# Causal attention in a hybrid decoder kernel: where the transposed queries, the keys and the values are split into two parts

## The chip, the core and the metric

The kernel runs on one core of a Trainium2 chip. A core has TensorE (matrix products and transposes, results in PSUM), VectorE, ScalarE and GpSimd (element-wise work), and SyncE, which issues DMAs here. The metric is the device time of one execution in microseconds. Before the change three runs took 1360.54 us in the median, 1357.71 to 1362.46.

## The reference

Two layers, 1024 tokens, model width 1024. In each layer one input projection feeds a convolution branch, an attention branch and a gated mixing branch; their outputs are gated, normalised, joined and projected. The change touches the attention alone:

```
def _causal_attention(q, k, v):          # 8 heads, q and k 96 wide, v 64 wide
    for each block of 128 queries:
        s = einsum(q_block, k) * Dq ** -0.5
        s = where(k_pos <= q_pos, s, -inf)
        p = softmax(s)
        out = einsum(p, v)
```

All arithmetic is float32. The kernel gets that from a TensorE format of less precision by writing an operand as hi + lo, hi being the rounded value and lo the rest (x - hi), and summing two or three products.

## The kernel before

The layers run one after the other. In a layer come the input projection with the convolution and mixing branches, the latent projections, keys and values per token (`ksb`, `vsb`), queries per token (`qsb`), attention head by head, and the output projection.

Attention of head h needs the queries and keys with their 96 channels on partitions. `qk_part` does it in four parts (keys or queries, first or second 512 tokens): four transposes on TensorE into a PSUM bank `qkt`, then the split into `qT` and `kT`. Before the change a part goes through three engines: ScalarE copies the bank to an SBUF tile `qkraw` (two buffers; L1022 for queries, L1024 with a gain for keys), VectorE casts `qkraw` to hi (L1025), GpSimd subtracts hi from `qkraw` for lo (L1026). `v_split` splits the 64 value columns of a head for all 1024 tokens into `vh`: VectorE casts hi (L1005), GpSimd subtracts (L1007).

Then `score` forms the scores `s` of a block of 128 queries in one of two double banks, VectorE takes the row maximum (L1050), ScalarE the exponential into `p` (L1056). `ptrans` transposes `p` into a bank `pt`, which ScalarE and VectorE split into `pT` (L169, L170): `pT_400` is head 4, first half of its queries, first 128 keys. `pv` sums the products with `vh` in a bank `o`; `os` (L1100, L1101) and `ot` bring the sum back to tokens. GpSimd also multiplies the gate `zsm` by one over the softmax's sum (L1076). The banks `qkt`, `pt`, `o` and `ot` come from one pool of four.

The order of the program is made by a planner in `attention`: it keeps a clock of TensorE and estimates (`est`) when ScalarE and VectorE are through, and takes up what it believes is ready. `t_ready` is when it believes a part of `qT` or `kT` to be usable. Work of the next head is placed between the scores of this one. The framework's scheduler may still move instructions of an engine past each other. On the chip every engine works off its own list in order.

Of the kernel before, what the change touches and what calls it, by code (L numbers as in the profile page):

```python
# [19 lines left out]
P = 128  # L20
# [21 lines left out]
# Columns of the input projection: where each part starts.  # L42
# [3 lines left out]
# Units of the input projection, in the order of their use.  # L46
# [15 lines left out]
# Pieces of the weight stream of a layer: (name, k chunks, columns).  # L62
# [11 lines left out]
# Columns of the per-partition parameters.  # L74
# [3 lines left out]
# Parameters that are rows, the same for all partitions.  # L78
# [3 lines left out]
# Columns of the constants.  # L82
# [4 lines left out]
class Flow:  # L87
    """Order of the program: work that waits for other engines is put off by as much
    tensor engine time as those take, so that engines, which run in order, find it ready."""
# [37 lines left out]
def hybrid_trunk(ctx, tc, x, w, pc, pr, sgw, pww, cst, out):  # L127
# [39 lines left out]
    def split(hi, lo, src):  # L167
        """hi + lo = src, for a source in PSUM."""
        nc.scalar.copy(hi, src)  # L169
        nc.vector.tensor_tensor(out=lo, in0=src, in1=hi.bitcast(F32), op=ALU.subtract)  # L170
# [63 lines left out]
    def late_splits():  # L234
        """Steps that split the pending pieces bit by bit."""
# [17 lines left out]
    class Unit:  # L253
        """A unit's weights: get(k) gives (hi, lo); in the last group, pieces are given back."""
# [38 lines left out]
    def s0_norm(l, i, xt, ng, pool, parts=1, dst=None):  # L293
        """RMSNorm of one tile of tokens, in place if there is no dst."""
# [13 lines left out]
    def to_chan(src, dst, t0, name, halves=1):  # L308
        """Transposes one tile of tokens, splits it into dst[:, part, k, t0:t0 + 128]."""
        chan_of([src[:, k * P:(k + 1) * P] for k in range(KC)], dst, t0, name, halves)  # L310
# [35 lines left out]
    # Products of zeros that bring the tensor engine to its full clock.  # L346
# [15 lines left out]
    # ================================================================ layers  # L362
    for l in range(L):
# [11 lines left out]
        def tok(o, un, i, n, final):  # L375
            """One tile of tokens times n columns of a unit."""
# [21 lines left out]
        def chan(un, c0, half, final, name):  # L398
            """128 channels of a unit times 512 tokens."""
# [145 lines left out]
        def silu2(o, dst, shape):  # L545
            """dst = 2 * silu(o)"""
# [5 lines left out]
        def branch_out(y, i0, c0):  # L552
            """Two tiles of a gated branch (twice its value): RMSNorm with gain, to DRAM."""
# [138 lines left out]
        # rotary tables with gains  # L692
# [12 lines left out]
        def key_prep():  # L705
            """Rotated key, sums of its squares."""
# [150 lines left out]
        def early_load(i):  # L857
            sd = t1p.tile([P, 512], F32, tag="qkraw", bufs=2, name="yse")
            side_load(i, sd[:, 0:CW], sd[:, CW:])
            early_src[i] = [sd]  # L860
# [7 lines left out]
        def open_t():  # L868
# [6 lines left out]
                  bank, bank2, mm, mm3, tr, split, ident_b, mask_b,  # L875
# [43 lines left out]
        def x_load(c, i):  # L919
            if c == 1 and not last:  # L920
                # The next layer's input: its first half is written, the second comes in place.
# [56 lines left out]
def attention(nc, flow, t1p, open_t, late_splits, extra, bank, bank2, mm, mm3, tr, split, ident_b, mask_b,  # L978
              ksb, qsb, vsb, zsm, kgain, early, l):
    """Causal softmax attention; the order of the tensor engine's work follows estimates of  # L980
    when the other engines are through with what it needs. Work of before (extra) fills the
    tensor engine while the first scores are on their way."""
# [19 lines left out]
    def v_split(h):  # L1002
        vh = vhs[h] = pool["t"].tile([P, NT, 2, DV], F32R, tag="vh", bufs=2, name=f"vh{l}_{h}")
        hc = vsb[:, :, h * DV:(h + 1) * DV]
        nc.vector.tensor_copy(vh[:, :, 0, :], hc)  # L1005
        est("dve", 0.35, flow.t)
        nc.gpsimd.tensor_tensor(out=vh[:, :, 1, :], in0=hc, in1=vh[:, :, 0, :].bitcast(F32),  # L1007
                                op=ALU.subtract)

    def qk_part(h, which, half):  # L1010
# [9 lines left out]
        raw = t1p.tile([P, 512], F32, tag="qkraw", bufs=2, name="qkraw")[:DQK, :]  # L1020
        if which == "q":
            nc.scalar.copy(raw, o[:DQK, :])  # L1022
        else:
            nc.scalar.activation(raw, o[:DQK, :], AF.Identity, scale=kgain)  # L1024
        nc.vector.tensor_copy(hi, raw)  # L1025
        nc.gpsimd.tensor_tensor(out=lo, in0=raw, in1=hi.bitcast(F32), op=ALU.subtract)  # L1026
        f = est("act", 0.55, flow.t)
        b1_free.remove(min(b1_free))
        b1_free.append(f)
        t_ready[h, which, half] = est("dve", 0.35, f) + (1.5 if h else 5.0)  # L1030
# [84 lines left out]
    # Sequence of scores and of the transposes that they need.  # L1115
# [21 lines left out]
    def s_when():  # L1137
# [3 lines left out]
        if kind != "s":  # L1141
            if "t" not in pool and h > 0:
                return None
            # The values of two heads before are read until its last product.
# [166 lines left out]
```

## Time and profile before

| | |
|---|---|
| three runs: median, lowest, highest | 1360.54, 1357.71, 1362.46 us |
| profiled execution: first to last instruction | 1356.9 us |
| what the runs have around that span | 0.8 us (lowest) to 5.6 us (highest), 3.6 us in the median |
| TensorE busy | 1281.4 us, 94% |
| VectorE, ScalarE, GpSimd busy | 855.7, 527.8, 536.8 us |
| attention of layer 0, of layer 1 | about 400 to 586 us, 1066 to 1258 us |

The profiled execution left no other time of its own than its span. Busy time is what an engine spent in instructions. PEclk is the granted clock of TensorE: 1.00 is 2.4 GHz and 0.50 is 1.2 GHz, the only two levels seen.

### The profile page before, as it was taken

Reading aid. Unit: us, or ns where it says so; the run is one execution under the profiler, and the core shown is the slowest. Engines: PE = TensorE matmul, PEld = TensorE weight load, DVE = VectorE, ACT = ScalarE, POOL = GpSimd, SP = SyncE. Lnnn points to the kernel's source line nnn. Section 1 sums busy time; section 2 is a strip of 40 time slices with the busy share of each in tenths; the row PEclk is TensorE's granted clock in tenths of the full one; section 3 lists DMA queues with packets and bytes.
Section 4 is the critical chain, followed back from the end, with each engine's and each line's share of the span. In section 5 each row is a group of like instructions: output and inputs, shape, how many; then the busy total and the mean of one; then the engine's idle time right before and its main releaser. Section 6 shows DMA issues by size and latency. Waiting matters only on the chain.

```text
span 1356.9 us, 19370 instructions
## 1 busy us (share of the span) xinstructions
PE 1281.4 (94%) x7566; PEld 1118.8 (82%) x7566; DVE 855.7 (63%) x1337; ACT 527.8 (39%) x1067; POOL 536.8 (40%) x468
## 2 busy tenths in 40 slices
PE   8999989999998989999999996999999898898998
PEld 7889879888987767778898996998889777777787
DVE  7499963124778877753555999621277877777431
ACT  6311333224346765630341211533243466566300
POOL 4724623543695333110055263344357833322100
PEclk9999989999998988999999997999999888889999
DMA  7121201211110000144432112111111100000332
GB/s 283 40 63 32 82 24 59 61 49 52 32 47 17 1 1 1 32 147 126 141 111 62 32 54 76 48 47 50 48 48 49 32 1 1 1 1 24 116 101 101
DMA packets 33820, 77.88 MB, mean 57 GB/s; under 512 B 3776, under 2 KB 12352, under 8 KB 33728
## 3 DMA queue, kind: packets, MB, share of 16 engines
q1 hardware_dynamic: 33728, 76.64, 17.9%
q8 instruction: 59, 0.97, 0.3%
q14 instruction: 33, 0.27, 0.1%
HBM read 64.05 MB, written 12.58 MB: 56 GB/s over the span
## 4 chain that ended last, share of the span: by engine, by line
PE 67%; DVE 24%; issue 4%; POOL 3%; ACT 2%; DMA 0%; SPq 0%; DVEq 0%; POOLq 0%
PE po L154 13%; DVE acc L517 13%; PE cq L154 10%; PE s L154 8%; PE o L154 6%; PE pt L165 4%; PE ckv L154 3%; PE pzk L154 3%; PE qps L154 3%; PE ZM L154 3%; PE V L154 2%; PE kps L154 2%; PE vps L154 2%; PE glu L154 2%; PE a L154 2%
## 5 line engine op out<-in xcount | busy, mean ns | idle before, releaser
L213 POOL TENSOR_TENSOR w<-raw,w 128x1024 fp32r<-128x1024 f32 (+1 forms) x49 | 137.3, 2809 | 149.6 <-ACT w L210 96.1
L154 PE MATMUL po<-w,yT 128*128 128x512 f32 x768 | 184.2, 398 | 0.0
L517 DVE SCALAR_TENSOR_TENSOR acc<-yp,dpc,acc 128x1024 f32<-128x1024 f32 x120 | 183.1, 1553 | 1.4
L154 PEld LDWEIGHTS po<-w,yT 128*128 128x128 f32 x768 | 142.9, 188 | 33.4
L154 PE MATMUL s<-kT,qT 96*128 96x384 f32 (+5 forms) x576 | 153.4, 394 | 5.4 <-ACT p L1056 5.4
L154 PE MATMUL o<-pT,vh 128*128 128x512 f32 (+3 forms) x384 | 127.8, 409 | 29.1 <-DVE pT L170 28.4
L154 PE MATMUL cq<-hT,w 128*128 128x512 f32 x576 | 132.0, 390 | 0.0
L154 PEld LDWEIGHTS cq<-hT,w 128*128 128x128 f32 x576 | 107.8, 188 | 22.2
L154 PEld LDWEIGHTS s<-kT,qT 96*128 96x128 f32 x576 | 104.1, 210 | 14.6 <-ACT p L1056 7.2
L170 DVE TENSOR_TENSOR pT<-pt,pT 128x512 fp32r<-128x512 f32 x192 | 101.1, 548 | 17.8 <-ACT pT L169 17.3
L169 ACT CAST pT<-pt 128x512 fp32r<-128x512 f32 x192 | 89.3, 478 | 58.2 <-PE pt L165 41.2
L1056 ACT ACTIVATE p<-s,rs 128x128 f32<-128x128 f32 (+7 forms) x128 | 94.9, 741 | 43.3 <-DVE rs L1050 38.6
L1050 DVE TENSOR_REDUCE rs<-s 128x1 f32<-128x128 f32 (+7 forms) x128 | 95.8, 749 | 24.8 <-PE s L154 23.2
L165 PE MATMUL pt<-cst_sb,p 128*128 128x128 f32 x576 | 99.2, 287 | 4.4 <-DVE pT L170 2.3
L154 PE MATMUL qps<-w,cqT 128*128 128x384 f32 x576 | 102.3, 337 | 0.0
L154 PEld LDWEIGHTS o<-pT,vh 128*128 128x128 f32 x384 | 69.7, 207 | 38.0 <-DVE pT L170 30.9
L154 PEld LDWEIGHTS qps<-w,cqT 128*128 128x128 f32 x576 | 100.2, 188 | 0.6
L1026 POOL TENSOR_TENSOR kT<-qkraw,kT 96x512 fp32r<-96x512 f32 x32 | 41.5, 1298 | 122.0 <-DVE kT L1025 122.0
L165 PEld LDWEIGHTS pt<-cst_sb,p 128*128 128x128 f32 x576 | 69.0, 148 | 13.1 <-ACT qkraw L1024 5.0
L174 DVE SCALAR_TENSOR_TENSOR cqT<-cq,pcs,cqT 128x512 fp32r<-128x512 f32 x24 | 18.0, 749 | 94.0 <-ACT cqT L173 94.0
L210 ACT CAST w<-raw 128x1024 fp32r<-128x1024 f32 (+1 forms) x47 | 49.6, 1057 | 49.9 <-PE a L154 14.9
L154 PE MATMUL ZM<-w,hT 128*128 128x256 f32 x384 | 53.1, 300 | 8.3 <-DVE zc L549 8.3
(306 smaller groups left out, 2374.5 us busy)
## 6 DMA issues: line engine op xcount, KB each, us to landing
raw<-in_w_dram SPq DMA_DIRECT2D x64, 512.0 KB, 3.5
raw<-in_w_dram SPq DMA_DIRECT2D x12, 576.0 KB, 3.7
xt<-in_x_dram SPq DMA_DIRECT2D x8, 512.0 KB, 8.2
xr<-xmid SPq DMA_DIRECT2D x16, 256.0 KB, 2.8
out_dram<-xr SPq DMA_DIRECT2D x16, 256.0 KB, 2.0
yn<-yside SPq DMA_DIRECT2D x24, 128.0 KB, 2.9
yside<-ug SPq DMA_DIRECT2D x8, 256.0 KB, 2.2
yside<-yc SPq DMA_DIRECT2D x8, 256.0 KB, 2.1
```

The lines of the kernel that those rows point to most:

```text
L154: nc.tensor.matmul(o, lhsT=lhsT, rhs=rhs, start=start, stop=stop)
L165: nc.tensor.transpose(out=o, in_=in_, identity=ident[:k, :k])
L169: nc.scalar.copy(hi, src)
L170: nc.vector.tensor_tensor(out=lo, in0=src, in1=hi.bitcast(F32), op=ALU.subtract)
L174: nc.vector.scalar_tensor_tensor(out=lo, in0=src, scalar=gain, in1=hi.bitcast(F32), op0=ALU.mult, op1=ALU.subtract)
L210: nc.scalar.copy(wt[:, 0, :sz], raw[:, :sz])
L213: (eng or nc.gpsimd).tensor_tensor(out=wt[:, 1, :sz], in0=raw[:, :sz], in1=wt[:, 0, :sz].bitcast(F32), op=ALU.subtract)
L517: nc.vector.scalar_tensor_tensor(out=acc, in0=yp[:, j:j + S], scalar=wc, in1=acc, op0=ALU.mult, op1=ALU.add)
L1026: nc.gpsimd.tensor_tensor(out=lo, in0=raw, in1=hi.bitcast(F32), op=ALU.subtract)
L1050: nc.vector.tensor_reduce(out=sm[:, 1, t:t + 1], in_=src if nb > 1 else o[:, :wd], axis=AX.XY if nb > 1 else AX.X, op=ALU.max, negate=True)
L1056: nc.scalar.activation(pr_[:, :n].rearrange("p (b n) -> p b n", b=nb), src, AF.Exp, bias=sm[:, 1, t:t + 1], accum_out=sm[:, 0, t:t + 1])
```

## The change

A query part is now split like `pT`: ScalarE copies the PSUM bank to hi, VectorE subtracts hi from the same bank for lo. A key part is split by the helper that the latents use, which applies the gain in both steps. `qkraw` is gone (its name tag on a later load becomes `yse`). For the values, ScalarE casts hi and VectorE subtracts; GpSimd has no part in the splits. The planner's estimates follow: the bank is taken to be free after VectorE, and `t_ready` has no margin of 1.5 (5.0 for head 0) any more.

```
     def v_split(h):
...
-        nc.vector.tensor_copy(vh[:, :, 0, :], hc)
-        est("dve", 0.35, flow.t)
-        nc.gpsimd.tensor_tensor(out=vh[:, :, 1, :], in0=hc, in1=vh[:, :, 0, :].bitcast(F32),
+        nc.scalar.copy(vh[:, :, 0, :], hc)
+        nc.vector.tensor_tensor(out=vh[:, :, 1, :], in0=hc, in1=vh[:, :, 0, :].bitcast(F32),
                                 op=ALU.subtract)
+        est("dve", 0.6, est("act", 0.55, flow.t))
...
     def qk_part(h, which, half):
...
-        raw = t1p.tile([P, 512], F32, tag="qkraw", bufs=2, name="qkraw")[:DQK, :]
         if which == "q":
-            nc.scalar.copy(raw, o[:DQK, :])
+            split(hi, lo, o[:DQK, :])
         else:
-            nc.scalar.activation(raw, o[:DQK, :], AF.Identity, scale=kgain)
-        nc.vector.tensor_copy(hi, raw)
-        nc.gpsimd.tensor_tensor(out=lo, in0=raw, in1=hi.bitcast(F32), op=ALU.subtract)
-        f = est("act", 0.55, flow.t)
+            split_gain(hi, lo, o[:DQK, :], kgain)
+        f = est("dve", 0.65, est("act", 0.55, flow.t))
         b1_free.remove(min(b1_free))
         b1_free.append(f)
-        t_ready[h, which, half] = est("dve", 0.35, f) + (1.5 if h else 5.0)
+        t_ready[h, which, half] = f
```

The helpers stood there before, and line 170 and line 174 are their VectorE steps:

```
    def split(hi, lo, src):
        nc.scalar.copy(hi, src)
        nc.vector.tensor_tensor(out=lo, in0=src, in1=hi.bitcast(F32), op=ALU.subtract)

    def split_gain(hi, lo, src, gain):
        nc.scalar.activation(hi, src, AF.Identity, scale=gain)
        nc.vector.scalar_tensor_tensor(out=lo, in0=src, scalar=gain, in1=hi.bitcast(F32),
                                       op0=ALU.mult, op1=ALU.subtract)
```

Behind the change the line numbers from 1022 on are three lower. Three places of the new order matter below. VectorE where head 4 passes to head 5, before the change:

```order
L1025 CAST kT_5_4598<-qkraw 96x512
L1050 TENSOR_REDUCE rs_5_0_4849<-s_5_0_4844 128x1
L1074 RECIPROCAL rs_4_7_4733<-rs_4_7_4733 128x4
L1005 CAST vh_5_4806<-vsb_2872 128x8x64
L1025 CAST qT_5_4597<-qkraw 96x512
L1050 TENSOR_REDUCE rs_5_0_4849<-s_5_1_4866 128x1
L170 TENSOR_TENSOR pT_400_4775<-pt_400_4768,pT_400_4775 128x512
```

The same place of VectorE with the change:

```order
L174 SCALAR_TENSOR_TENSOR kT_5_4558<-qkt_5k_4693,dpc_353,kT_5_4558 96x512
L1047 TENSOR_REDUCE rs_5_0_4799<-s_5_0_4794 128x1
L1071 RECIPROCAL rs_4_7_4689<-rs_4_7_4689 128x4
L170 TENSOR_TENSOR qT_5_4557<-qkt_5q_4711,qT_5_4557 96x512
L1047 TENSOR_REDUCE rs_5_0_4799<-s_5_1_4816 128x1
L170 TENSOR_TENSOR pT_400_4727<-pt_400_4720,pT_400_4727 128x512
L1098 TENSOR_TENSOR os<-o_31_4622,os 64x512
L1006 TENSOR_TENSOR vh_5_4758<-vsb_2872,vh_5_4758 128x8x64
```

The two casts of keys and queries have become subtractions from PSUM, and the work on the values has moved behind `pT_400`. TensorE at this place, from behind the last product of head 3 on, before the change:

```order
L165 MATMUL pt_401_4785<-cst_sb,p_4_1_4614 128x128
L165 MATMUL pt_401_4785<-cst_sb,p_4_2_4654 128x128
L165 MATMUL pt_401_4785<-cst_sb,p_4_3_4674 128x128
L154 MATMUL s_5_1_4866<-kT_5_4598,qT_5_4597 128x256 x3
L154 LDWEIGHTS ident_b
L154 MATMUL s_5_1_4866<-mask_b,ident_b 128x128
L165 MATMUL pt_402_4820<-cst_sb,p_4_2_4654 128x128
L165 MATMUL pt_402_4820<-cst_sb,p_4_3_4674 128x128
L154 MATMUL s_5_2_4906<-kT_5_4598,qT_5_4597 128x384 x3
L154 LDWEIGHTS ident_b
L154 MATMUL s_5_2_4906<-mask_b,ident_b 128x128
L154 MATMUL o_40_4828<-pT_400_4775,vh_4_4549 128x512 x2
```

The same place of TensorE with the change:

```order
L154 MATMUL s_5_1_4816<-kT_5_4558,qT_5_4557 128x256 x3
L154 LDWEIGHTS ident_b
L154 MATMUL s_5_1_4816<-mask_b,ident_b 128x128
L165 MATMUL pt_401_4751<-cst_sb,p_4_1_4572 128x128
L165 MATMUL pt_401_4751<-cst_sb,p_4_2_4604 128x128
L165 MATMUL pt_401_4751<-cst_sb,p_4_3_4619 128x128
L165 MATMUL pt_402_4774<-cst_sb,p_4_2_4604 128x128
L165 MATMUL pt_402_4774<-cst_sb,p_4_3_4619 128x128
L154 MATMUL o_40_4780<-pT_400_4727,vh_4_4509 128x512 x2
L154 MATMUL s_5_2_4848<-kT_5_4558,qT_5_4557 128x384 x3
```

The score `s_5_2`, which stood ahead of the first product of head 4 (`o_40`), stands behind it now. The third place is VectorE at the start of layer 0's attention, before the change:

```order
L1005 CAST vh_0_3668<-vsb_2872 128x8x64
L1025 CAST qT_1_3671<-qkraw 96x512
L1025 CAST kT_1_3672<-qkraw 96x512
L1005 CAST vh_1_3784<-vsb_2872 128x8x64
L170 TENSOR_TENSOR pT_000_3763<-pt_000_3756,pT_000_3763 128x512
```

The same place with the change:

```order
L1006 TENSOR_TENSOR vh_0_3660<-vsb_2872,vh_0_3660 128x8x64
L170 TENSOR_TENSOR qT_1_3663<-qkt_1q_3665,qT_1_3663 96x512
L174 SCALAR_TENSOR_TENSOR kT_1_3664<-qkt_1k_3688,dpc_353,kT_1_3664 96x512
L174 SCALAR_TENSOR_TENSOR kT_1_3664<-qkt_1k_3715,dpc_353,kT_1_3664 96x512
L170 TENSOR_TENSOR qT_1_3663<-qkt_1q_3733,qT_1_3663 96x512
L1006 TENSOR_TENSOR vh_1_3768<-vsb_2872,vh_1_3768 128x8x64
L1047 TENSOR_REDUCE rs_0_7_3711<-s_0_5_3740 128x1
L170 TENSOR_TENSOR pT_000_3758<-pt_000_3751,pT_000_3758 128x512
```

Six subtractions and a row maximum stand ahead of the first `pT` there, where four casts stood.

## Rows read from the trace of the kernel before

**Rows 1.** The page's first and fourth part: busy engines, chain that ended last.

```profile
PE 1281.4 (94%) x7566; PEld 1118.8 (82%) x7566; DVE 855.7 (63%) x1337; ACT 527.8 (39%) x1067; POOL 536.8 (40%) x468
...
PE 67%; DVE 24%; issue 4%; POOL 3%; ACT 2%; DMA 0%; SPq 0%; DVEq 0%; POOLq 0%
```

**Rows 2.** Windows between the first products of successive heads, engines' busy time, granted clock.

```profile
core 0: us, PE busy (x) PEld busy (x) DVE busy (x) ACT busy (x) POOL busy (x), PEclk, DMA share, GB/s
437.20:459.65 22.45, 20.05 (x136) 16.63 (x136) 18.63 (x35) 17.00 (x42) 9.64 (x10) 1.00 0.00 1
459.65:480.77 21.12, 18.72 (x128) 15.54 (x128) 17.97 (x32) 15.11 (x34) 7.70 (x8) 1.00 0.00 1
480.77:505.03 24.26, 21.85 (x128) 17.89 (x128) 17.97 (x32) 15.12 (x34) 7.69 (x8) 0.86 0.00 1
...
1154.62:1177.30 22.68, 20.27 (x128) 16.42 (x128) 17.96 (x32) 15.12 (x34) 7.70 (x8) 0.92 0.00 1
```

**Rows 3.** TensorE's waits, layer 0 then 1: total us, times, longest.

```profile
PE o L154 <- DVE pT L170: 13.0, 7, 2.4
...
PE ot L165 <- DVE os L1101: 1.4, 1, 1.4
...
PE o L154 <- DVE pT L170: 15.4, 9, 2.4
```

**Rows 4.** Timeline, head 4 to 5: start, us, engine, work, idle before it.

```profile
500.01 0.42 DVE L1025 CAST kT<-qkraw 96x512 fp32r<-96x512 f32 x1 [0.53 <-ACT qkraw L1024]
...
500.56 0.29 DVE L1050 TENSOR_REDUCE rs<-s 128x1 f32<-128x128 f32 x1
500.65 0.57 ACT L1022 COPY qkraw<-qkt_5q 96x512 f32<-96x512 f32 x1
...
501.06 1.01 DVE L1005 CAST vh<-vsb 128x512 fp32r<-128x512 f32 x1
...
501.75 0.79 POOL L1076 TENSOR_TENSOR zsm<-zsm,rs 128x256 f32<-128x256 f32 x1
501.78 0.77 PE L154 MATMUL s<-kT,qT 96*128 96x384 f32 x3
502.00 2.05 DVE L1025 CAST qT<-qkraw 96x512 fp32r<-96x512 f32 x1
...
502.51 1.26 POOL L1007 TENSOR_TENSOR vh<-vsb,vh 128x512 fp32r<-128x512 f32 x1
...
503.97 0.41 DVE L1050 TENSOR_REDUCE rs<-s 128x1 f32<-128x256 f32 x1
...
504.30 0.67 DVE L170 TENSOR_TENSOR pT<-pt,pT 128x512 fp32r<-128x512 f32 x1
...
505.03 0.91 PE L154 MATMUL o<-pT,vh 128*128 128x512 f32 x3 [2.41 <-DVE pT L170]
```

**Rows 5.** Line 1025, casts of queries: shortest, median and longest in ns.

```profile
L1025 DVE CAST qT<-qkraw x32: 411/423/2053, 380.2 to 1223.0; 96x512 fp32r<-96x512 f32 x32
```

**Rows 6.** Groups by line and form, whole span: busy us, mean ns, idle before.

```profile
L170 DVE TENSOR_TENSOR pT<-pt,pT 128x512 fp32r<-128x512 f32 x96 | 65.2, 685 | 17.2 <-ACT pT L169 16.7
L174 DVE SCALAR_TENSOR_TENSOR cqT<-cq,pcs,cqT 128x512 fp32r<-128x512 f32 x24 | 18.0, 749 | 94.0 <-ACT cqT L173 94.0
...
L768 DVE TENSOR_TENSOR ksb<-ksb,kst 128x512 f32<-128x512 f32 x16 | 11.0, 686 | 3.8 <-POOL kst L178 3.8
...
L447 ACT CAST vn<-vg 128x512 fp32r<-128x512 f32 x8 | 5.0, 621 | 28.3 <-POOL vg L443 24.1 <-DVE rstd L425 4.2
```

**Rows 7.** Timeline, start of layer 0's attention.

```profile
410.90 0.42 DVE L1005 CAST vh<-vsb 128x512 fp32r<-128x512 f32 x1
...
414.43 1.14 DVE L170 TENSOR_TENSOR pT<-pt,pT 128x512 fp32r<-128x512 f32 x2
415.16 0.69 PE L165 MATMUL pt<-cst_sb,p 128*128 128x128 f32 x2 [2.29 <-DVE pT L170]
```

**Rows 8.** Window behind layer 0's wait for `os`, columns as in Rows 2.

```profile
580.00:600.00 20.00, 18.00 (x95) 14.56 (x94) 13.47 (x24) 8.49 (x20) 4.09 (x7) 1.00 0.51 157
```

More of the change, by code (lines that the diff above doesn't have):

```diff
@@ L857, in early_load @@
         def early_load(i):
-            sd = t1p.tile([P, 512], F32, tag="qkraw", bufs=2, name="yse")
+            sd = t1p.tile([P, 512], F32, tag="yse", bufs=2, name="yse")
             side_load(i, sd[:, 0:CW], sd[:, CW:])
@@ L874, in hybrid_trunk @@
         attention(nc, flow, t1p, open_t, late_splits, [lambda i=i: query(1, i) for i in range(2, NT)],
-                  bank, bank2, mm, mm3, tr, split, ident_b, mask_b,
+                  bank, bank2, mm, mm3, tr, split, split_gain, ident_b, mask_b,
                   ksb, qsb, vsb, zsm, dpc[:DQK, 66:67], (early_load, early_norm), l)
@@ L975, in hybrid_trunk, with attention @@
             hT, cs = nhT, ncs
-def attention(nc, flow, t1p, open_t, late_splits, extra, bank, bank2, mm, mm3, tr, split, ident_b, mask_b,
+def attention(nc, flow, t1p, open_t, late_splits, extra, bank, bank2, mm, mm3, tr, split, split_gain, ident_b, mask_b,
               ksb, qsb, vsb, zsm, kgain, early, l):
```

## The prediction

> **What bounds the kernel now.** The page comes first: TensorE is busy for 94% of the span and carries 67% of the chain that ended last, VectorE 24% of it [rows 1]. So the place to look for is where TensorE waits, and what its clock does there. The change lies in attention, so the waits of TensorE were read for the two attention stretches alone: nearly all is one kind, products `o` waiting for VectorE's half of `pT`, 13.0 and 15.4 us, the longest 2.4 us [rows 3]. Eleven waits of 2.40 to 2.42 us, one at each passage from head to head, make 26.5 of those 28.4 us. The timeline of one passage [rows 4] shows what VectorE does meanwhile: a cast of the values that lasts 1.01 us beside GpSimd's work on `zsm`, then a cast of queries that lasts 2.05 us while GpSimd subtracts for `vh`. The usual cast of this form takes 0.423 us [rows 5]. The first `pT` stands behind both, and TensorE idles from 502.62 to 505.03.
>
> The windows by head [rows 2] show a second loss. A head of 128 products takes 21.12 us at a granted clock of 1.00 (2.4 GHz) with 18.72 us of TensorE work; heads with the same work take 24.26 us at 0.86. There are seven like this one (24.2 to 24.5 us), each with some 2 x 0.14 x 24.26 = 6.8 us at the level 0.50, and three with half as much (0.92; 22.68 us here, the other two being the last heads of the layers). Ten of the eleven long waits were followed by such a stretch. A wait of 0.60 us ahead of 437.20 was not (clock 1.00 in the head after it [rows 2]), nor the wait of 1.39 us for `os` in the window of 580 to 600 [rows 3, 8].
>
> **The change part by part.**
>
> *VectorE's work.* In the head of [rows 4] the five casts cost 2.05 + 1.01 + 3 x 0.42 = 4.32 us. After it there are two query subtractions from PSUM, priced as the `pT` subtraction, 0.685 us (512 columns too; that only 96 partitions take part is taken not to matter), two key subtractions as the gained split of the latents, 0.749, and one for the values as line 768, a product with 512 columns in SBUF, 0.686 [rows 6]: 3.55 us, 0.8 less. Outside the passage VectorE gets more: 0.27 to 0.33 us for each part whose cast ran undisturbed.
>
> Here a rule speaks against the change. The Trainium skill ("VectorE: DVE Perf Modes", Mode 2x_2P) says that a copy with one source, from SBUF to SBUF, may run two elements per cycle even in fp32, and that a tensor_tensor or a source in PSUM can't. The rows bear it out for undisturbed casts: 0.423 us against 0.685. By undisturbed prices alone the splits would cost VectorE more: 64 parts and 16 value splits at 0.423 are 33.8 us, the new ones 32 x 0.685 + 32 x 0.749 + 16 x 0.686 = 56.9 us, so 23.0 us more. By the rows of the passage they cost less, since the two casts that stand beside GpSimd are the slow ones and GpSimd has no part in the splits any more. I go by the passage, and keep the 23.0 us for a rival.
>
> *The passage.* I walk [rows 4] in the new order, from 500.01, when the key part's hi is ready on ScalarE in either kernel. Keys 0.749 and row maximum 0.29 bring VectorE to 501.05. ScalarE's copy of the queries ends at 501.22, and a short reciprocal fits in between; query subtraction 0.685, row maximum 0.41, `pT_400` 0.67: done at 502.99. That is 1.98 us earlier than 504.97. Instructions of VectorE start up to 0.08 us before the one ahead ends in these rows, so 502.9 is as likely. TensorE gets there earlier too: `s_5_2`, from 501.78 to 502.62, now stands behind `o_40`, so it arrives at 501.78. The wait left is 1.1 us where it was 2.41. Bounds: 0.5 us if TensorE is itself held up ahead of it; 1.7 us if `o_40` gets the bank of `o_31`, which is free only after `os` (0.6 us more). I take 1.1, since each bank that is needed before (`pt_401`, `pt_402`) is given back by the key and query subtractions before TensorE comes. Eleven passages x 1.3 us: 14.3 us less (7.8 to 21).
>
> *The clock.* With the granted clock at 1.00 the seven heads would each lose 24.2 - 21.12 = 3.08 us, the three with half a stretch 22.68 - 21.12 = 1.56 us: 26.2 us. A wait of 1.1 us lies between 0.60 and 1.39, behind which the clock stayed at 1.00, and well below 2.4. I take the whole 26.2; the other end is nothing.
>
> *ScalarE.* Each head gets one cast of values, 0.621 us [rows 6], on 15.1 us of work in 21.12 [rows 2]. It stands behind the `pT_400` and `os` copies, and what it delays is `p_5_0`, the exponential that frees the bank for `s_5_2`. With the copies of query and `pT_400` after 500.65, `os`, values and that exponential, ScalarE frees it at about 503.4, when TensorE, started at 503.0 with two products of 0.3 us, needs it at 503.6. So nothing, up to 0.6 us for each passage.
>
> *GpSimd* loses 80 subtractions of about 1.27 us and keeps `zsm`. What this gives VectorE is counted at the passage; by itself it is worth nothing, as no other engine's step at the passage waits for a subtraction of GpSimd.
>
> *Tighter heads.* If a head takes 18.72 + 1.1 us, VectorE has 17.97 - 0.8 = 17.2 us of work in 19.8: 87% instead of 85% in the fast head. I add 0.3 us of new short waits for each of the twelve heads behind a passage (the eleven and that of 437.20), 3.6 us (0 to 10).
>
> *The start.* Ahead of the first `pT` stood four casts, 410.90 to 414.43 [rows 7]. Now there are six subtractions, 2 x 0.685 + 2 x 0.749 + 2 x 0.686 = 4.2 us, and a row maximum, so that the first `pT` comes 1.5 to 2 us later. But `pt_002`, and the two parts of head 1 that VectorE did after it, are then done. The wait of 2.29 us stays and so does the slow stretch behind it. I take 0, between -2.3 and +2 us for each layer.
>
> **The sum.** -14.3 - 26.2 + 3.6 = -36.9 us. The profiled execution had a span of 1356.9 us, so 1320.0; the median of the runs is 3.6 us above that span, which gives 1323.6 us, in round numbers 1323.
>
> **Rivals.**
>
> *The clock falls all the same.* One slow stretch in a head needs only a wait that is still long enough. For it: nothing in the rows lies between 1.39 and 2.29 us, and if the bank of `o_31` decides the wait is 1.7 us. Against: the two shorter waits above. Then -14.3 + 3.6 = -10.7 us, 1350 us.
>
> *VectorE becomes the limit: slower.* This is the rule above as a mechanism. The bank of every `qkt` part is now held until VectorE is through instead of ScalarE, and VectorE's queue is longer away from the passages. If TensorE's transposes wait for VectorE at each of the 56 parts of heads 1 to 7 in both layers, the loss is 56 times that wait; with the clock at its old level it passes the 14.3 us won from 0.26 us on. At the undisturbed price, 23.0 us more and nothing won at the passage, the time is 1384 us. For it: VectorE's 85%. Against: VectorE was busy all through the wait of 2.41 us, so in the other 18.7 us of the fast head it was at 15.56, 83%, and TensorE hardly waited there; and at the passage the casts are slow by waiting, not by work.
>
> *Nothing moves.* The wait is only handed on: ScalarE, with the values' cast and hi parts that nobody staged, is late with `pT_400` by the 2 us that VectorE gains. Then 1360 us. Against: the walk has that copy done at about 501.8, 0.5 us before VectorE wants it.
>
> **How the numbers follow.** The forecast has 0.64, with a range of its own of 1308 to 1340 (passages 7.8 to 21, new waits 0 to 10, start -4.6 to +4). The clock that falls all the same has 0.17, VectorE as the limit 0.11, nothing moved 0.08. A measurement of this kernel tells 0.3% (4 us) from no change. So faster 0.64 + 0.17 = 0.81, same 0.08, slower 0.11. To leave out no more than 2 in 10 the range takes in the second case and reaches from 1302 to 1354.
>
> **What would show it.** In the profile after, waits of `o` for `pT` of about 1.1 us in place of 2.4; heads of about 20 us at a clock of 1.00; no VectorE split over 0.8 us; key subtractions near 0.75 and query subtractions near 0.69; the same start. It would be wrong if query subtractions from 96 partitions took far longer than 0.69, if TensorE's transposes wait for banks, or if heads still show 0.86.

## The result and the profile after

The changed kernel takes 1318.7 us in the median of four runs (1318.5 to 1319.34), the kernel before 1361.43 us in four runs beside them (1357.71 to 1362.46). The ratio is 0.9697, with a 95% interval of 0.968 to 0.9714. The profiled execution's span went from 1356.9 to 1316.9 us, 40.0 us less.

The page's first and fourth part, busy engines and the chain that ended last (compare [rows 1]):

```profile
PE 1258.1 (96%) x7566; PEld 1099.6 (84%) x7566; DVE 835.6 (63%) x1337; ACT 532.4 (40%) x1083; POOL 431.4 (33%) x388
...
PE 69%; DVE 21%; ACT 4%; issue 3%; POOL 1%; DMA 0%; SPq 0%; ACTq 0%; DVEq 0%; POOLq 0%
```

TensorE has 23.3 us less busy time for the same number of instructions: they ran at a higher clock. GpSimd has 105 us less. VectorE's share of the chain fell from 24% to 21%, and its busy time by 20 us, though the prices of undisturbed instructions would have given it 23 us more.

Windows between the first products of successive heads in the changed kernel, then layer 0's start, columns as in [rows 2]:

```profile
457.37:477.45 20.08, 19.40 (x128) 15.78 (x128) 16.66 (x32) 15.33 (x36) 1.23 (x2) 1.00 0.01 2
477.45:497.53 20.08, 19.39 (x129) 15.76 (x129) 16.67 (x32) 15.35 (x36) 1.22 (x2) 1.00 0.00 1
...
1125.76:1145.86 20.10, 19.41 (x129) 15.76 (x129) 16.68 (x32) 15.36 (x36) 1.22 (x2) 1.00 0.00 1
...
400.00:420.00 20.00, 14.19 (x80) 11.47 (x79) 15.37 (x29) 12.08 (x29) 8.29 (x14) 0.83 0.18 54
```

Three heads of each layer take 20.1 us at the full clock, where they took 21.12 at 1.00, 22.68 at 0.92 or 24.2 at 0.86. Of the two others that the table below counts, one takes 21.0 us and one 20.2. In attention the low clock is left only at the start of each layer.

TensorE's waits in layer 0's attention (total us, times, longest; compare [rows 3]):

```profile
PE pt L165 <- DVE qT L170: 5.4, 7, 4.2
PE o L154 <- DVE pT L170: 2.8, 7, 0.4
PE s L154 <- ACT p L1053: 2.0, 5, 0.9
PE ot L165 <- DVE os L1098: 1.4, 1, 1.4
```

The products' waits for `pT` fell from 13.0 us to 2.8, none over 0.43. A new kind stands first: transposes `pt` wait for a query subtraction. One of them, 4.2 us, is at the start; the others are short.

The passage from head 4 to head 5, timeline (compare [rows 4]):

```profile
494.61 0.75 DVE L174 SCALAR_TENSOR_TENSOR kT<-qkt_5k,dpc,kT 96x512 fp32r<-96x512 f32 x1 [0.28 <-ACT kT L173]
...
495.25 0.57 ACT L169 CAST qT<-qkt_5q 96x512 fp32r<-96x512 f32 x1
...
495.72 0.61 POOL L1073 TENSOR_TENSOR zsm<-zsm,rs 128x256 f32<-128x256 f32 x1 [13.36 <-DVE rs L1071]
495.86 0.69 DVE L170 TENSOR_TENSOR qT<-qkt_5q,qT 96x512 fp32r<-96x512 f32 x1 [0.21 <-ACT qT L169]
...
496.46 0.41 DVE L1047 TENSOR_REDUCE rs<-s 128x1 f32<-128x256 f32 x1
...
496.69 0.41 PE L165 MATMUL pt<-cst_sb,p 128*128 128x128 f32 x2 [0.20 <-DVE qT L170]
496.79 0.68 DVE L170 TENSOR_TENSOR pT<-pt,pT 128x512 fp32r<-128x512 f32 x1
...
497.53 0.73 PE L154 MATMUL o<-pT,vh 128*128 128x512 f32 x2 [0.43 <-DVE pT L170]
```

VectorE goes from the key part to the end of `pT` in 2.86 us (494.61 to 497.47) where it took 4.96 before (500.01 to 504.97). GpSimd still works on `zsm` in the middle of it, and no instruction of VectorE is longer for it.

The start of layer 0's attention, timeline (compare [rows 7]):

```profile
405.39 0.58 ACT L169 CAST qT<-qkt_1q 96x512 fp32r<-96x512 f32 x1
...
406.64 1.09 DVE L1047 TENSOR_REDUCE rs<-s 128x1 f32<-128x896 f32 x1 [0.43 <-PE s L154]
...
407.65 0.55 DVE L810 TENSOR_TENSOR qsb<-qsb,qs 128x384 f32<-128x384 f32 x1
...
408.27 0.60 POOL L813 TENSOR_TENSOR t<-qsb,tab 128x64 f32<-128x64 f32 x2 [1.07 <-DVE qsb L810]
408.91 0.29 DVE L818 TENSOR_TENSOR qsb<-qsb,tab 128x128 f32<-128x128 f32 x1 [0.71 <-POOL t L813]
...
409.23 0.29 DVE L819 TENSOR_TENSOR qsb<-qsb,t 128x128 f32<-128x128 f32 x1
409.44 0.68 DVE L1006 TENSOR_TENSOR vh<-vsb,vh 128x512 fp32r<-128x512 f32 x1
...
410.04 0.68 DVE L170 TENSOR_TENSOR qT<-qkt_1q,qT 96x512 fp32r<-96x512 f32 x1
...
410.78 1.54 PE L165 MATMUL pt<-cst_sb,p 128*128 128x128 f32 x6 [4.18 <-DVE qT L170]
```

ScalarE has the query part's hi at 405.97, but VectorE subtracts only at 410.04. Of these 4.07 us VectorE works 2.9, on what stands ahead in its list: row maxima, the rotation of queries (L810 to L819) and the subtraction for the values. It idles 0.43 us for scores and 0.71 for GpSimd's products of the rotation (L813), for which GpSimd itself had to wait for L810. The bank stays taken until then, and TensorE's transposes wait 4.18 us for one. Before, the first long wait there was the 2.29 us of [rows 7].

Where the 40.0 us of span went, by windows at the same places in both kernels (granted clock in brackets). The five heads begin with the first product of the second head, at 437.20 and 1106.22 us before and at 436.39 and 1084.73 after:

| stretch | before | after | change |
|---|---|---|---|
| up to the end of TensorE's first wait for `p` in layer 0 | 403.4 | 402.3 | -1.1 |
| layer 0's start, from there to the five heads | 33.8 (0.85) | 34.1 (0.90) | +0.3 |
| five heads of layer 0 | 116.53 (0.91) | 101.46 (1.00) | -15.1 |
| last part of layer 0, output and inputs of layer 1 | 515.4 | 513.2 | -2.2 |
| layer 1's start | 37.11 (0.86) | 33.68 (0.95) | -3.4 |
| five heads of layer 1 | 119.79 (0.87) | 101.47 (1.00) | -18.3 |
| rest | 130.9 | 130.7 | -0.2 |

The windows of the two starts, layer 0 then 1, first before, then after:

```profile
403.44:437.20 33.76, 30.06 (x169) 24.64 (x169) 27.49 (x48) 21.25 (x48) 19.44 (x22) 0.85 0.11 32
1069.11:1106.22 37.11, 31.36 (x177) 25.20 (x177) 30.38 (x51) 23.19 (x55) 21.27 (x24) 0.86 0.10 29
```

```profile
402.31:436.39 34.08, 28.23 (x170) 23.20 (x170) 27.06 (x48) 23.36 (x52) 6.72 (x12) 0.90 0.11 32
1051.05:1084.73 33.68, 28.21 (x170) 22.86 (x170) 26.84 (x48) 23.40 (x52) 6.71 (x12) 0.95 0.11 32
```

The splits themselves took what the new lines were expected to take, here those of head 5 (shortest, median and longest in ns):

```profile
L170 DVE TENSOR_TENSOR qT<-qkt_5q,qT x4: 687/687/687, 482.0 to 1144.2; 96x512 fp32r<-96x512 f32 x4
```

```profile
L174 DVE SCALAR_TENSOR_TENSOR kT<-qkt_5k,dpc,kT x4: 731/740/747, 486.8 to 1142.9; 96x512 fp32r<-96x512 f32 x4
```

### The profile page after: what moved, and what is told of

The parts are those of the page before. It is cut to its first block, busy times and chain, and to the rows that moved or that the text cites. A ratio compares the mean times of both kernels' runs of the same rounds, so it can differ in the third digit from the quotient of the medians.

```text
span 1316.9 us, 19326 instructions
## 1 busy us (share of the span) xinstructions
PE 1258.1 (96%) x7566; PEld 1099.6 (84%) x7566; DVE 835.6 (63%) x1337; ACT 532.4 (40%) x1083; POOL 431.4 (33%) x388
## 4 chain that ended last, share of the span: by engine, by line
PE 69%; DVE 21%; ACT 4%; issue 3%; POOL 1%; DMA 0%; SPq 0%; ACTq 0%; DVEq 0%; POOLq 0%
PE po L154 14%; DVE acc L517 13%; PE cq L154 10%; PE s L154 8%; PE qps L154 7%; PE o L154 5%; PE ckv L154 3%; PE pt L165 3%; PE pzk L154 3%; PE ZM L154 3%; PE V L154 2%; PE kps L154 2%; PE vps L154 2%; PE glu L154 2%; PE a L154 2%
## 5 line engine op out<-in xcount | busy, mean ns | idle before, releaser
L154 PE MATMUL s<-kT,qT 96*128 96x384 f32 (+5 forms) x576 | 133.1, 358 | 3.7 <-ACT p L1053 3.7
L154 PEld LDWEIGHTS s<-kT,qT 96*128 96x128 f32 x576 | 95.5, 192 | 17.3 <-ACT p L1053 9.8
L1073 POOL TENSOR_TENSOR zsm<-zsm,rs 128x256 f32<-128x256 f32 x32 | 19.6, 612 | 275.6 <-DVE rs L1071 275.6
L1047 DVE TENSOR_REDUCE rs<-s 128x1 f32<-128x128 f32 (+7 forms) x128 | 95.6, 748 | 15.9 <-PE s L154 15.3
L165 PE MATMUL pt<-cst_sb,p 128*128 128x128 f32 x576 | 94.3, 278 | 10.7 <-DVE qT L170 10.7
L154 PEld LDWEIGHTS o<-pT,vh 128*128 128x128 f32 x384 | 65.2, 192 | 17.1 <-DVE pT L170 10.3
```

The source lines that it names most:

```text
L154: nc.tensor.matmul(o, lhsT=lhsT, rhs=rhs, start=start, stop=stop)
L165: nc.tensor.transpose(out=o, in_=in_, identity=ident[:k, :k])
L1047: nc.vector.tensor_reduce(out=sm[:, 1, t:t + 1], in_=src if nb > 1 else o[:, :wd], axis=AX.XY if nb > 1 else AX.X, op=ALU.max, negate=True)
L1073: nc.gpsimd.tensor_tensor(out=z, in0=z, in1=sm[:, 2, :].unsqueeze(2).broadcast_to([P, 4, DV]), op=ALU.mult)
```

## The experiments

Ten kernels ran, each against the kernel before on the same chip; a ratio below is to that kernel. What stood open was which part of the change brings the gain, whether GpSimd or VectorE's own work made the long wait, whether the clock hangs on that wait, and what the planner's figures do.

**1. Queries and keys alone.** The changed kernel with the values split as before.

```
-        nc.scalar.copy(vh[:, :, 0, :], hc)
-        nc.vector.tensor_tensor(out=vh[:, :, 1, :], in0=hc, ...)
-        est("dve", 0.6, est("act", 0.55, flow.t))
+        nc.vector.tensor_copy(vh[:, :, 0, :], hc)
+        est("dve", 0.35, flow.t)
+        nc.gpsimd.tensor_tensor(out=vh[:, :, 1, :], in0=hc, ...)
```

> The change for queries and keys alone; the values are split by VectorE (cast) and GpSimd (subtraction) as before. Theory A (VectorE's casts waited for GpSimd): only the cast of the values still lies beside GpSimd, 0.42 to 0.8 us ahead of the first pT of a head, so the wait at a passage is 0.43 + 0.4 to 0.8 us, the clock stays at 1.00: 1319 to 1328 us, 1324 likeliest. Theory B (only VectorE's amount of work counts): near 1318, since VectorE has about as much to do. Theory C (the planner's order made the gain): near 1319, too.

Measured: 1317.26 us, ratio 0.9666 (0.9637 to 0.9694), span 1315.4. That is the whole gain. The shortest heads take 20.0 us, and the waits at the passages are 0.40 us (0.86 at one), now of transposes for the bank of a query part. The group of the values' casts, by line and form (busy us, mean ns, idle before):

```profile
L1005 DVE CAST vh<-vsb 128x512 fp32r<-128x512 f32 x16 | 7.1, 452 | 0.8
```

The cast that took 1.01 us in [rows 4] is back to 0.45 us in the mean, since with the 64 subtractions for queries and keys gone GpSimd is seldom at work when it comes.

**2. Values alone.** The kernel before with the new split of the values, the same lines the other way round.

> The change for the values alone; queries and keys are staged, cast by VectorE and subtracted by GpSimd as before, with the planner's old numbers for them. Theory A: the cast of queries at the passage lies beside the keys' subtraction and the zsm product of GpSimd only, so it ends 1.1 to 1.8 us earlier than before; the wait at a passage is 0.5 to 1.3 us and the clock stays up: 1322 to 1335 us, 1328 likeliest. Theory B: VectorE wins 0.3 us a head, 1355 us. Theory C: 1350 us or more, the old margins being in place.

Measured: 1319.24 us, ratio 0.9687 (0.9659 to 0.9716), span 1317.6. This is the whole gain too. TensorE's waits for `pT` in layer 0, then the groups of the query casts and of the values' subtractions:

```profile
PE o L154 <- DVE pT L170: 2.9, 7, 0.5
```

```profile
L1025 DVE CAST qT<-qkraw 96x512 fp32r<-96x512 f32 x32 | 19.9, 622 | 8.6 <-ACT qkraw L1022 8.5
...
L1006 DVE TENSOR_TENSOR vh<-vsb,vh 128x512 fp32r<-128x512 f32 x16 | 13.0, 810 | 0.0
```

The query casts are still slower than the undisturbed 423 ns. But none reaches 2 us (the longest took 902 ns), since no subtraction of GpSimd for the values comes between, and the wait left is 0.5 us. The values' subtraction takes 670 to 674 ns in 14 of 16 cases, as in the changed kernel; two of 1.77 us, one at each layer's start, make its mean. So the two halves of the change don't add up: either one breaks the chain of cast, GpSimd, cast at the passage, and behind the wait that is left the clock did not fall.

**3. The planner's old figures** with the changed kernel's engines.

```
-        f = est("dve", 0.65, est("act", 0.55, flow.t))
+        f = est("act", 0.55, flow.t)
...
-        t_ready[h, which, half] = f
+        t_ready[h, which, half] = est("dve", 0.35, f) + (1.5 if h else 5.0)
```

> The changed kernel with the planner's old numbers (bank free after ScalarE, margins of 1.5 and 5.0 in t_ready, the old figure for the values). Theory A: 1316 to 1328 us, since the engines do the same work. Theory C: most of the gain is gone, 1340 us or more.

Measured: 1319.22 us, ratio 0.9683 (0.9651 to 0.9715), span 1318.2. The three heads that took 20.1 us take some 19.6, half a microsecond less than in the changed kernel, and the kernel is no faster; runs 9 and 10 come back to that.

**4. Parts of head 1 later.** In the changed kernel, the four parts of head 1 are placed among the later scores of head 0, the values behind them.

```
+            if h == 0:
+                nx = {7: ("k", 1, 0), 6: ("q", 1, 0), 5: ("k", 1, 1), 4: ("q", 1, 1)}
             for i in SORD:
                 sq.append(("s", h, i))
+                if h == 0 and i == 4:
+                    sq.append(("v", 1, 0))
```

> The changed kernel, but the four query and key parts of head 1 are asked for after the scores of blocks 7, 6, 5 and 4 of head 0 instead of after blocks 0, 2, 6 and 7, and the values of head 1 last. Theory: the wait of 4.2 us at the start of each layer's attention comes from banks that hold parts of head 1 until VectorE takes them; with fewer of them ahead of the first pt the wait falls to 1 to 3 us and with it the slow stretch behind it: 1310 to 1317 us. Rival: VectorE's queue at the start is what lasts, and the wait only moves: 1317 to 1321 us.

Measured: 1319.87 us, ratio 0.9688 (0.9661 to 0.9715), span 1318.0. The wait at the start only changed its name; TensorE's longest wait in layer 0 is now:

```profile
PE qkt_1q L165 <- DVE kT L174: 3.9, 1, 3.9
```

So it isn't a matter of which bank is asked for first: in either order the work ahead in VectorE's list lasts about as long, and TensorE waits for it.

**5. All the subtractions to VectorE, staging kept.** The kernel before, with two engine names changed.

```
-        nc.gpsimd.tensor_tensor(out=vh[:, :, 1, :], in0=hc, ...)
+        nc.vector.tensor_tensor(out=vh[:, :, 1, :], in0=hc, ...)
...
-        nc.gpsimd.tensor_tensor(out=lo, in0=raw, ...)
+        nc.vector.tensor_tensor(out=lo, in0=raw, ...)
```

> The kernel before with every subtraction of the query, key and value splits moved from GpSimd to VectorE; the staging copy, the casts and the planner's numbers stay. VectorE gets 80 subtractions more. Theory A: no GpSimd subtraction lies beside a cast, casts last 0.42 us (0.8 beside the zsm product), the wait at a passage falls to 0.5 to 1.2 us, the clock stays up, and the head is 20 to 21 us: 1322 to 1350 us, 1335 likeliest. Theory B (VectorE's work): 80 x 0.69 us more with 2.2 us a head given back, about 19 us slower than before: 1380 us.

Measured: 1334.02 us (1328.31 to 1337.76), ratio 0.9807 (0.9779 to 0.9834). The profiled execution is the fastest of the four, span 1326.5. VectorE has 80 casts and 80 subtractions here, and 866 us of busy time on the page where the kernel before has 856; the time still fell. The groups of its splits, then TensorE's largest wait in layer 0:

```profile
L1026 DVE TENSOR_TENSOR qT<-qkraw,qT 96x512 fp32r<-96x512 f32 x32 | 21.8, 682 | 0.2
...
L1025 DVE CAST kT<-qkraw 96x512 fp32r<-96x512 f32 x32 | 13.4, 418 | 5.1 <-ACT qkraw L1024 5.1
...
L1005 DVE CAST vh<-vsb 128x512 fp32r<-128x512 f32 x16 | 6.4, 400 | 0.0
```

```profile
PE s L154 <- ACT p L1056: 8.7, 11, 1.3
```

Casts of keys and values are undisturbed, those of queries take 0.83 us at the passages, beside `zsm`, and what TensorE waits for is the exponential. This separates the two readings of the 2.41 us: it was GpSimd beside the casts and not the quantity of VectorE's work. That work is not free either: the heads that take 20.2 us in layer 0 take 21.9 in layer 1, and why they differ was not tried.

**6. Only the values' subtraction to VectorE**, the first of the two changes of run 5.

> The kernel before with one engine name changed: VectorE instead of GpSimd subtracts for the values. Theory A: the cast of queries ends after the zsm product (about 502.8 on the old time scale) instead of after GpSimd's value subtraction (504.05), but VectorE then has 0.69 us more ahead of the first pT, unless that is placed behind it: the wait at a passage is about 1.9 us and the clock still falls: 1345 to 1360 us. Theory B: 0.3 to 0.7 us more a head: 1365 to 1372 us.

Measured: 1342.16 us, ratio 0.9858 (0.9837 to 0.9879), span 1342.6. The wait at ten passages is 1.78 to 1.80 us instead of 2.41, and behind five of the ten the clock still fell. VectorE at one of them:

```profile
500.96 0.83 DVE L1025 CAST qT<-qkraw 96x512 fp32r<-96x512 f32 x1
501.72 0.68 DVE L1007 TENSOR_TENSOR vh<-vsb,vh 128x512 fp32r<-128x512 f32 x1
```

The query cast takes 0.83 us instead of 2.05, which is 1.22 less, and the moved subtraction stands ahead of the first `pT`, some 0.6 us more: 2.41 - 1.22 + 0.6 = 1.79. So less of GpSimd's work beside the casts gives a shorter wait even with more work for VectorE, and a shorter wait fewer falls of the clock.

**7. GpSimd's subtractions again, unused.** In the changed kernel GpSimd does 80 subtractions of the old shapes, whose results nobody reads. Those for queries and keys read hi twice and take 1.07 us in the mean, where the old ones took 1.29.

```
             split_gain(hi, lo, o[:DQK, :], kgain)
+        jk = t1p.tile([P, 512], F32, tag="yse", bufs=2, name="junk")
+        nc.gpsimd.tensor_tensor(out=jk[:DQK, :], in0=hi.bitcast(F32), in1=hi.bitcast(F32), op=ALU.subtract)
```

> The changed kernel with the 80 GpSimd subtractions of before put back at their places, each on the same shape and from SBUF, with results that nobody reads. Theory A: VectorE's subtractions read PSUM and one SBUF operand and are not held up by GpSimd; only the values' subtraction with two SBUF operands may be, behind the first pT: within 3 us of the changed kernel, 1318 to 1322 us. Rival: any GpSimd work beside VectorE costs, then 1335 us or more.

Measured: 1325.78 us, ratio 0.9739 (0.9721 to 0.9756), span 1323.5. TensorE's waits in layer 0, the values' subtractions (shortest, median and longest in ns), then VectorE at the start of layer 0's attention:

```profile
PE pt L165 <- DVE qT L170: 8.0, 7, 6.8
PE o L154 <- DVE pT L170: 2.8, 7, 0.4
```

```profile
L1006 DVE TENSOR_TENSOR vh<-vsb,vh x16: 673/675/1685, 411.1 to 1193.3; 128x512 fp32r<-128x512 f32 x16
```

```profile
408.77 1.34 DVE L818 TENSOR_TENSOR qsb<-qsb,tab 128x128 f32<-128x128 f32 x1 [0.71 <-POOL t L813]
410.14 1.01 DVE L819 TENSOR_TENSOR qsb<-qsb,t 128x128 f32<-128x128 f32 x1
411.07 1.52 DVE L1006 TENSOR_TENSOR vh<-vsb,vh 128x512 fp32r<-128x512 f32 x1
```

Nothing happens at the passages: the heads take 142.92 us from the first `ot` to the last in layer 0, as against 142.98. The span's 6.6 us come ahead of that, 2.7 us up to layer 0's first `ot` and 4.1 from its last to layer 1's first, where the wait at the start grew from 4.2 to 6.8 us in both layers. These 2.6 us are three instructions of VectorE with both inputs in SBUF, which had 0.29, 0.29 and 0.68 us in the changed kernel and are 1.05, 0.72 and 0.84 us longer beside GpSimd. Subtractions from PSUM keep their duration. The values' subtraction from SBUF is long in four of 16 cases (1.52 and 1.69 us, two at each layer's start); in the others it keeps 673 to 676 ns, and at the passages it is GpSimd's subtraction of the same values that takes 2.24 us. The Trainium skill ("SBUF — State Buffer", Who interferes with whom) says that a VectorE instruction with two inputs from SBUF contends with a GpSimd instruction that reads SBUF, and one with at most one such input, outside the two-port modes, does not. The rows agree on both. Casts that can go two elements at a time are blocked whole, it says there; the 2.05 us of [rows 4] look like that, and no run measured a lone pair of a cast and a GpSimd instruction.

**8. VectorE late at the passage.** The changed kernel with an unused maximum over a bank, read five times over (2.82 us), ahead of the second query part from head 1 on.

```
         if which == "q":
+            if half and h:
+                jk = t1p.tile([P, 2], F32, tag="yst", bufs=4, name="junk")
+                nc.vector.tensor_reduce(out=jk[:DQK, 0:1],
+                                        in_=o[:DQK, :].unsqueeze(1).broadcast_to([DQK, 5, 512]),
+                                        axis=AX.XY, op=ALU.max)
             split(hi, lo, o[:DQK, :])
```

> The changed kernel with one maximum over a PSUM bank, read five times over, on VectorE ahead of the key or query split at each passage from head 1 on (about 2.7 us, its result unused); the scheduler moves the query split behind the first pT, so the first pT comes about 2 us later. If the whole loss of before was the late first pT and the clock behind it, the time comes near the one of before: 12 x 2 + 26 = 50 us more would be 1369, with the clock falling at only half of the passages 1355 us: 1345 to 1372 us. If the clock is not tied to these waits: 1340 to 1345 us, heads at 1.00.

Measured: 1365.39 us, ratio 1.0023 (1.0006 to 1.0039), span 1363.4. TensorE's largest wait in layer 0, then three windows from wait to wait:

```profile
PE pt L165 <- DVE kT L174: 12.0, 6, 2.1
```

```profile
463.93:489.78 25.85, 23.75 (x128) 19.03 (x129) 19.51 (x34) 15.79 (x35) 1.23 (x2) 0.81 0.00 1
489.78:513.02 23.24, 20.99 (x128) 16.78 (x129) 19.49 (x34) 15.79 (x35) 1.23 (x2) 0.93 0.01 1
...
536.39:558.70 22.31, 19.50 (x128) 15.79 (x129) 19.34 (x34) 15.68 (x35) 1.23 (x2) 1.00 0.00 1
```

A wait of 2.09 to 2.10 us at each of the eleven passages, made without GpSimd, brings the loss of the kernel before back, with the low clock at eight of them.

**9. The old figures behind head 0 only.** As run 3, with no margin for head 0 in place of 5.0.

```
-        t_ready[h, which, half] = est("dve", 0.35, f) + (1.5 if h else 5.0)
+        t_ready[h, which, half] = est("dve", 0.35, f) + (1.5 if h else 0.0)
```

> The changed kernel with the planner's old figures for the two split halves (ScalarE 0.55 us, then VectorE 0.35 us, and 1.5 us of margin) behind head 0, and no margin for head 0; the values are planned at 0.35 us on VectorE alone. Engines and data as in the changed kernel. Theory A (what is left per head, 20.08 us against some 19.5 in the run with all the old figures, is a question of where the planner puts the parts, and the late start of the run with all the old figures came from the margin of 5 us at head 0): heads near 19.6 us, 10 heads by 0.5 us = 5 us less than the changed kernel, the start as there: 1313 to 1316 us. Theory B (what the heads win is given back at the start or in the stretch between, since the order there changes with the same figures): heads near 19.6 us, the start or the weights behind it later by as much, 1317 to 1320 us.

Measured: 1320.65 us, ratio 0.9716 (0.9702 to 0.9731), span 1319.8. A window of a head (from an `ot` to the same one of the next head), and the 31 us from the last `ot` of layer 0 on; under them those 31 us in the changed kernel:

```profile
481.77:501.33 19.56, 18.93 (x129) 15.52 (x129) 16.83 (x33) 15.46 (x35) 1.23 (x2) 1.00 0.00 1
569.83:600.87 31.04, 31.04 (x150) 25.54 (x151) 15.77 (x24) 9.84 (x19) 3.70 (x6) 0.95 0.58 176
```

```profile
568.96:600.00 31.04, 31.04 (x157) 25.63 (x158) 16.00 (x24) 9.84 (x19) 3.70 (x6) 1.00 0.59 177
```

The heads are shorter, as theory A has it, and the time is not, as theory B has it. From the first `ot` of a layer to its last the run is 1.4 and 2.4 us shorter than the changed kernel. It loses 2.3 us up to the first `ot`, 2.8 from layer 0's last `ot` to layer 1's first, and 1.6 behind layer 1's last. Much of that is clock: behind the last wait for `os` (1.39 us in both kernels) it falls here and not in the changed kernel, 0.05 x 31.04 = 1.6 us in layer 0, and the 1.6 us behind layer 1 are of the same size (the stretch to the end has 0.98 for 0.99). Layer 1's start, with the same wait of 4.17 us, has 0.90 over 34.5 us here and 0.95 over 33.7 in the changed kernel, some 1.7 us more. So the comparison does not say what the planner's figures alone are worth over the whole span.

**10. The same with the values split as before.**

> As the run before it, with the values split as in the kernel before (cast on VectorE from SBUF, subtraction on GpSimd). Theory A (the values' subtraction on GpSimd meets no cast on the path now, and relieves ScalarE and VectorE by 0.62 + 0.67 us per half-head pair): 1 to 2 us below the run before it, 1312 to 1315 us. Theory B (VectorE's cast of the values is blocked by GpSimd's scaling of zsm, as before the change): waits of 1 us or more at passages, 1318 to 1325 us.

Measured: 1317.06 us, ratio 0.9692 (0.9677 to 0.9706), span 1316.4. Theory B's waits of 1 us at passages don't come, and theory A's 1312 to 1315 isn't reached. Its interval overlaps those of the changed kernel and of run 1. No version here is faster than the changed kernel by more than the measurement tells.

## Why the prediction was right, and where its terms were off

**The forecast held.** 1318.7 us lies 4.3 below the 1323 predicted, and inside the likeliest case's own 1308 to 1340. The mechanism is the one given: the blocked casts at the passage made the wait, the wait brought the low clock, and both go. Runs 1, 2, 5 and 6 show the first (less of GpSimd's work beside the casts, less wait), run 8 the second. The span is 3.1 us below the 1320.0 of the sum. The rest is the 3.6 us that the sum adds for what a run has around its span: it set the span of one execution against the median of others, and each run of the changed kernel is only 1.7 to 1.8 us above its own span.

**The passage** was mis-sized: 2.41 became 0.43 us and not 1.1, so 11 x 1.98 = 21.8 us instead of 14.3, just past the end of the range given (7.8 to 21). (One of the eleven became 0.29.) VectorE's side of the walk was right (2.98 us from the key part to the end of `pT` predicted, 2.86 measured). The steps that failed are on TensorE's side: it gets to its product at 497.10, 2.49 us after VectorE starts on the key part, where the walk had 1.77, and so it waits less. About a third of the 0.72 us is in the walk itself. It has TensorE free at 501.78, when `s_5_2` started, but the transposes ahead end at 502.03 in the kernel before:

```profile
501.64 0.39 PE L165 MATMUL pt<-cst_sb,p 128*128 128x128 f32 x2
```

Another 0.20 us is "each bank that is needed before is given back before TensorE comes": `pt` waits 0.20 us for the query subtraction's bank. The rest was not taken apart. What the passage wins by TensorE's coming later is lost ahead of the wait.

**New waits in the heads** were the opposite error. A head would take 21.12 - 1.98 = 19.14 us if the wait were all; it takes 20.08, so 0.94 us more, some 9 us over the ten heads of the windows, where 0.3 per head was put down. TensorE's busy time in the head of [rows 2] rose from 18.72 to 19.40 us, so most of it lies in products that start and are held, not in waits that the views list. Run 9 (19.56 us, 18.93 busy) shows that half of it is the planner's new figures. The other half wasn't taken apart. The two errors nearly cancel, which is luck: 18.72 + 1.1 + 0.3 = 20.12 was predicted for a head.

**The clock.** All ten heads of the table have 1.00 now, and the price put on them holds: the seven slow heads and one of the three with half a stretch are 7 x 3.08 + 1.56 = 23.1 us, and with ten waits shorter by 1.98 us and 9.4 us of new waits that makes 33.5 us less, where the table has 33.4. The other 3.1 us of the 26.2 were put on the last head of each layer. Its clock came back from 0.90 to 1.00 too, but it takes 17.56 us for 17.73 in layer 0 and 17.55 for 17.70 in layer 1.

**The start** was taken as nothing, with "the wait of 2.29 us stays and so does the slow stretch behind it". Neither stayed. The first long wait is 4.18 us, for a bank: the rival on banks held until VectorE is through, in the place where most of VectorE's other work stands ahead of the split. Run 7 shows the price, some 6.6 us for 2.6 us more wait in each layer. The windows of the starts show what paid for it: the clock took some 5 us of each start before, and takes 3.4 and 1.7 us of them now. Layer 0's start came out 0.3 us longer, layer 1's 3.4 shorter, the latter with one passage's wait in it. That the term came near nothing is luck. The 1.1 us up to there is a wait for `p` that went from 1.90 to 0.48 us; the same wait, from 1.90 to 0.54 us, is 1.4 of the 2.2 us ahead of layer 1's start. Why `p` comes earlier there was not tried.

**The rivals.** The clock that falls all the same did not come, but run 6 shows how near it was: at 1.8 us it fell behind half of the waits, so with the 1.7 us that the text held possible it might have. The argument against it was weaker than it looked at both ends. "Nothing in the rows lies between 1.39 and 2.29 us" holds of the rows shown; the trace of the kernel before has waits of 1.90 us for `p` ahead of 403.44 and 1069.11, with the low clock behind both, here the first:

```profile
403.44:410.29 6.85, 6.05 (x25) 4.16 (x25) 4.80 (x7) 2.50 (x6) 5.42 (x10) 0.75 0.51 155
```

And 1.39 us is no safe length: the wait of 1.39 us for `os` comes twice in each of the twelve kernels profiled here, and behind ten of the 24 the clock fell. VectorE as the limit fell: split prices are as predicted (query 673 to 689 ns, key 731 to 749), so VectorE did get the longer instructions that undisturbed prices give, but the casts they replace had cost it more: 64.6 us (32.7, 16.6 and 15.3 for queries, keys and values), and the subtractions 56.3. Run 5 shows that even more of them cost less than GpSimd beside the casts. "Nothing moves" fell with the time; ScalarE's new cast of the values costs nothing that run 1 against the changed kernel would show (ratios 0.9666 and 0.9697, with intervals that overlap). GpSimd's step, "by itself it is worth nothing", holds at the passages once VectorE's casts are gone, and not at the start (run 7).

**What the prediction didn't see** is that each half of the change alone is enough (runs 1 and 2). It priced the two slow casts as a pair, and the pair is the point: one cast stands behind GpSimd's instruction, lets the next one start late, and that one stands behind GpSimd's next. It also took the wrong partner for the first. The cast of the values was read as standing beside `zsm`, but GpSimd was at the key subtraction when it began:

```profile
500.51 1.28 POOL L1026 TENSOR_TENSOR kT<-qkraw,kT 96x512 fp32r<-96x512 f32 x1 [5.40 <-DVE kT L1025]
```

The cast ends at 502.07, 0.28 us behind that subtraction, and the query cast at 504.05, 0.28 us behind the one for the values. The same holds for all 30 casts over 0.7 us in the two attentions of the kernel before: each ends 0.28 or 0.29 us behind a GpSimd instruction that it overlapped. So run 1, which leaves no key subtraction, and run 2, which leaves none for the values, each take one link out.

## What to carry to other kernels

When a cheap VectorE instruction shows a few very long cases, look what GpSimd does beside those cases, and cost the change by them and not by the mean or the undisturbed price. A wait of TensorE costs its length and, if it is long enough, the clock behind it, so first remove what makes the longest wait; the smallest edit that breaks its chain may give the whole gain. Take bank hold times into the walk of TensorE too: a split that reads PSUM twice moves the wait from the reader of the result to the next user of the bank.

## What the runs showed of the hardware

- The same wait can be followed by the low clock or not. 1.78 to 1.80 us: it fell behind five of ten (run 6). 2.09 to 2.10 us: the windows behind show 0.81, 0.93 and 1.00, and it fell at eight of eleven (run 8). 1.39 us behind the last products of attention: 1.00 in the changed kernel and 0.95 over 31 us in run 9, and it fell behind ten of 24 in all kernels profiled. Prices for such a loss are therefore a count of cases and not a rule.
- A cast of the splits on VectorE, from SBUF to SBUF with 512 columns, takes 0.40 to 0.42 us in the mean where GpSimd does not meet it (values and keys in run 5). Each of the 30 that took over 0.7 us in the kernel before (0.79 to 2.05 us) ended 0.28 or 0.29 us behind a GpSimd instruction that it overlapped.
- A subtraction on VectorE with both inputs in SBUF takes 670 to 684 ns in the changed kernel. With GpSimd's subtractions there it was longer in two of 16 cases in run 2, six in run 6 and four in run 7, by 0.3 to 1.1 us, and kept 670 to 677 ns in the others. The subtractions from PSUM of the same length keep 673 to 689 ns in the kernel after and 671 to 689 in run 7.
- On GpSimd the values' subtraction of the old shape took 1.27 us in the mean in run 1, and the unused one of run 7 mostly 2.24 us, beside VectorE's subtraction of the same values.
